# A filler tile in SBUF grows from 192 to 224 bytes per partition, in an fp32r two-layer encoder trunk on one core

## The chip, the cores and the metric

The kernel runs on one core of a Trainium2 chip. The metric is the device time of one execution in microseconds; lower is better. Three runs of the kernel before took 2316.77, 2317.53 and 2318.99 us; their median is 2317.53 us.

## The reference

Two layers of a hybrid block work on 512 frames of width 1024, and a final RMSNorm follows. Each layer normalizes the frames and multiplies them by one wide input matrix. Its columns go to an mLSTM branch (4 heads), a retention branch (4 heads) and two branch gates. The branches are merged and projected; then come a feed-forward part with a squared relu and a gated embedding:

```python
for i in range(DEPTH):
    h = rmsnorm(x, norm1_g[i])
    z = h @ w_in[i] + b_in[i]
    ...                                   # conv, mLSTM and retention, each with its output gate
    merged = jax.nn.sigmoid(gm) * (y_m @ w_bm[i]) + jax.nn.sigmoid(gr) * (y_r @ w_br[i])
    x = x + merged @ w_out[i]
    h2 = rmsnorm(x, norm2_g[i])
    x = x + jnp.square(jax.nn.relu(h2 @ w_ff1[i] + b_ff1[i])) @ w_ff2[i] + b_ff2[i]
    h3 = rmsnorm(x, norm3_g[i])
    x = x + jax.nn.sigmoid(h3 @ w_pe_gate[i]) * (p[i] @ w_pe[i])
return rmsnorm(x, final_g)
```

All of it is float32. The change leaves the computation alone.

## The kernel before

Activations lie with their 1024 features on partitions, in eight tiles of 128 x 512 frames. Every operand of a large product is split into a high part that fp32r holds exactly and a low part (`split`, lines 302 to 304: ScalarE writes the high part, VectorE subtracts it for the low part). Each product is then three matmuls: high by high, high by low, low by high (`mm3`, lines 479 to 482).

The weights arrive as raw pieces `wr` of 128 x 1024 float32 (four buffers), and are split into `wh` and `wl` (six buffers, and two for half-size pieces `wh_D` and `wl_D`). There are four ways in which they are used:

- `t8` (lines 480 to 482): a piece holds eight 128 x 128 blocks. Each block is loaded as TensorE's weights, and a 128 x 512 activation tile is the moving operand. So a matmul has 512 columns.
- `values` (lines 799 to 801): the activations are loaded and 512 columns of the weight piece move.
- `run_pair` (lines 531 to 533): a scheme with seven products in place of eight, on halves of 256 frames. The weights are loaded, 256 columns of activations move. The moving operand is either an activation tile itself or one of the sums that the scheme needs.
- `run_wide` (lines 575 to 577): the same scheme with the operands' roles exchanged. The activations or their sums are loaded, 512 columns of a weight piece move.

A `LDWEIGHTS` on TensorE loads the 128 x 128 operand of the next matmul while a matmul runs; the profile calls it PEld. Most sums of weight pieces are formed in DRAM by transfers that accumulate, issued on GpSimd's queue at a pace tied to the matmuls. Loads of weight pieces go through SP's queue in the order of use.

SBUF is allocated from two ends. The pools of the whole kernel are opened first, on the left (low addresses), in this order:

```python
cpool = pool("const", 1)
cols = pool("cols", 2)
padp = pool("pad", 1)
padp.tile([P, PAD], F32, name="pad")
wpool = pool("w", PIECES)
bpool = pool("big", 1)
opool = pool("one", 1)
```

`pad` is a tile that no instruction touches. The constants and columns end at byte 5,408 of each partition. With `PAD` = 48 floats, 192 bytes, the weight pool begins at 5,600, which is 224 bytes past a multiple of 256. All raw and split pieces are 4,096 or 2,048 bytes long, so each begins 224 bytes past a multiple of 256. So do the tiles of `big` and `one` behind them.

Above them lie the pools of the phases, on the left or on the right (line 976): in layer 0 the activations of a phase (`n1`, `xs`, `n2`, `ns`, `n3`) are on the right, and the working pools (queries and keys, values, `ym`, `yr`, `mh`, the hidden tiles) on the left; in layer 1 it is the other way round. `x`, the high part of the normalized activations `xnh`, and in layer 1 `nsh` lie in `big`, on the left; the low part `xnl` lies in the working pool. The right end of SBUF's allocation is byte 229,344, also 224 past a multiple of 256, and nearly all tiles are multiples of 256 bytes long. So almost every tile on either side begins at 224.

The exception is made by `shift` (lines 275 to 278): it puts a filler of 64 bytes below the sums `xs` and below the feed-forward pool where these are on the left, and one of 192 bytes into the pool where they are on the right. By it the sums `xs` (the moving operand of `l0r`, `l0bgm`, `l0gr` and their like in layer 1, and the loaded operand in the wide units), the hidden tiles `hh` and `hl` (moving in `l0o` and `l1o`) and the embedding's `pth` and `ptl` (moving in `l0pe`) begin 32 bytes past a multiple of 256.

Names in the profile: `l0f` is layer 0's first feed-forward product as whole tiles, `l0f13a` and its like the same product by pairs, `l0o` the second feed-forward product, `l0bm`, `l0br` and `l0wo` the merge and its projection, `l0pg` the gate of the embedding, `l0m` and `l0r` the mLSTM and the retention, `l0g` the retention's output gates.

Of the kernel before, what the change touches and what calls it, by code (L numbers as in the profile page):

```python
# [56 lines left out]
NTMP = 6  # L57
RAWS = 4
PIECES = 3
PAD = 48  # L60
LAST = 4
SIGN = (1.0, -1.0)

# [189 lines left out]
def build(ctx, tc, ins, out):  # L253
# [5 lines left out]
    def pool(name, bufs, **kw):  # L259
        return ctx.enter_context(tc.tile_pool(name=name, bufs=bufs, **kw))  # L260
# [6 lines left out]
# [3 lines that stand above are left out]
# [1531 lines left out]
```

## Time and profile before

| | |
|---|---|
| runs, us | 2316.77, 2317.53, 2318.99; median 2317.53 |
| profiled execution: span, first to last instruction, us | 2313.4 |
| profiled execution: time outside the span | the page gives none |
| instructions | 36,468 |
| TensorE matmul (PE) | 2299.1 us, 99%, 13,532 matmuls |
| TensorE weight load (PEld) | 2035.4 us, 88%, 13,532 loads |
| VectorE (DVE) | 1766.8 us, 76% |
| ScalarE (ACT) | 1269.6 us, 55% |
| GpSimd (POOL) | 624.1 us, 27% |
| granted TensorE clock, mean | 0.998 |
| transfers | 499.36 MB, 187,603 packets, 216 GB/s |

The profile was taken on one execution. Matmuls overlap: one is listed as lasting from its first row to its modelled end, some 390 ns with 512 columns, while the next begins 227 ns after it. So what a matmul costs is read from start to start, and not from its listed duration. Weight loads are listed as PEld. A row of waits names the waiting engine and tile, what it waited for, the total in us, the number of waits and the longest one.

### The profile page before, as it was taken

Reading aid. Unit: us, or ns where it says so; the run is one execution under the profiler, and the core shown is the slowest. Engines: PE = TensorE matmul, PEld = TensorE weight load, DVE = VectorE, ACT = ScalarE, POOL = GpSimd, SP = SyncE. Lnnn points to the kernel's source line nnn. Section 1 sums busy time; section 2 is a strip of 40 time slices with the busy share of each in tenths; the row PEclk is TensorE's granted clock in tenths of the full one; section 3 lists DMA queues with packets and bytes.
Section 4 is the critical chain, followed back from the end, with each engine's and each line's share of the span. In section 5 each row is a group of like instructions: output and inputs, shape, how many; then the busy total and the mean of one; then the engine's idle time right before and its main releaser. Section 6 shows DMA issues by size and latency. Waiting matters only on the chain.

```text
span 2313.4 us, 36468 instructions
## 1 busy us (share of the span) xinstructions
PE 2299.1 (99%) x13532; PEld 2035.4 (88%) x13532; DVE 1766.8 (76%) x2690; ACT 1269.6 (55%) x1837; POOL 624.1 (27%) x984
## 2 busy tenths in 40 slices
PE   9999999999999999999999999999999999999998
PEld 8888899888898899999888888988888888999997
DVE  7878767886676878788778777778867678787785
ACT  6756544644554546556557564445445446566564
POOL 4333222223124322223442332221231242111112
PEclk9999999999999999999999999999999999999999
DMA  7776787777789888888886768877877898878851
GB/s 218 189 191 174 238 228 216 215 227 210 232 230 261 220 228 223 240 239 215 222 224 182 196 174 247 232 216 216 223 221 208 241 266 218 247 232 228 232 160 55
DMA packets 187603, 499.36 MB, mean 216 GB/s; under 512 B 26064, under 2 KB 29520, under 8 KB 187424
## 3 DMA queue, kind: packets, MB, share of 16 engines
q0 software_dynamic: 57520, 188.53, 37.1%
q1 hardware_dynamic: 114496, 281.06, 36.6%
q10 hardware_dynamic: 15408, 27.43, 3.5%
q8 instruction: 106, 1.74, 0.3%
q14 instruction: 73, 0.60, 0.1%
HBM read 478.05 MB, written 194.51 MB: 291 GB/s over the span
## 4 chain that ended last, share of the span: by engine, by line
PE 92%; DVE 5%; ACT 1%; issue 1%; DMA 1%; POOL 0%; SPq 0%; ACTq 0%; DVEq 0%; POOLq 0%
PE l0br L480 1%; PE l1br L480 1%; PE l1br L481 1%; PE l0br L482 1%; PE l1br L482 1%; PE l0br L481 1%; PE l0f L480 1%; PE l0f L481 1%; PE l0f L482 1%; PE l1f L480 1%; PE l1f L481 1%; PE l1f L482 1%; PE l0pg L480 1%; PE l1bm L480 1%; PE l0pg L482 1%
## 5 line engine op out<-in xcount | busy, mean ns | idle before, releaser
L303 ACT ACTIVATE wh<-wr 128x1024 fp32r<-128x1024 f32 (+1 forms) x193 | 199.7, 1041 | 140.5 <-issue 17.1
L304 DVE TENSOR_TENSOR wl<-wr,wh 128x1024 fp32r<-128x1024 f32 (+1 forms) x191 | 234.6, 1230 | 37.5 <-ACT wh L303 36.9
L303 ACT ACTIVATE wh_B<-wr 128x1024 fp32r<-128x1024 f32 x123 | 130.3, 1059 | 184.5 <-PE l0br L481 15.7
L304 DVE TENSOR_TENSOR wl_B<-wr,wh_B 128x1024 fp32r<-128x1024 f32 x123 | 150.3, 1222 | 55.1 <-ACT wh_B L303 50.6
L303 ACT ACTIVATE wh_C<-wr 128x1024 fp32r<-128x1024 f32 x75 | 79.2, 1056 | 69.5 <-PE l0br L481 8.3
L304 DVE TENSOR_TENSOR wl_C<-wr,wh_C 128x1024 fp32r<-128x1024 f32 x75 | 91.7, 1223 | 21.3 <-ACT wh_C L303 17.1
L303 ACT ACTIVATE wh_A<-wr 128x1024 fp32r<-128x1024 f32 x75 | 78.9, 1052 | 44.3 <-DMA wr<-wpairs 5.2
L304 DVE TENSOR_TENSOR wl_A<-wr,wh_A 128x1024 fp32r<-128x1024 f32 x75 | 91.6, 1221 | 12.6 <-ACT wh_A L303 9.4
L303 ACT ACTIVATE wh_D<-wr 128x512 fp32r<-128x512 f32 x75 | 47.2, 630 | 96.5 <-DVE wr L462 27.3
L303 ACT ACTIVATE wh_t<-wr 128x1024 fp32r<-128x1024 f32 x56 | 59.4, 1061 | 69.0 <-PE l0g2va L576 6.0
L304 DVE TENSOR_TENSOR wl_t<-wr,wh_t 128x1024 fp32r<-128x1024 f32 x56 | 68.2, 1221 | 26.1 <-ACT wh_t L303 25.5
L304 DVE TENSOR_TENSOR wl_D<-wr,wh_D 128x512 fp32r<-128x512 f32 x75 | 51.8, 690 | 30.2 <-ACT wh_D L303 28.7
L480 PE MATMUL l0f<-l0n2h,wh 128*128 128x512 f32 x176 | 68.7, 390 | 0.0
L481 PE MATMUL l0f<-l0n2l,wh 128*128 128x512 f32 x176 | 68.6, 390 | 0.0
L482 PE MATMUL l0f<-l0n2h,wl 128*128 128x512 f32 x176 | 68.5, 389 | 0.0
L361 POOL DMA_DIRECT2D s30t<-wpairs x24 | 16.8, 699 | 92.4 <-PE l1o11a L533 9.4
L482 PEld LDWEIGHTS l0f<-l0n2h,wl 128*128 128x128 f32 x176 | 33.0, 188 | 7.0
L480 PEld LDWEIGHTS l0f<-l0n2h,wh 128*128 128x128 f32 x176 | 33.1, 188 | 6.6
L481 PEld LDWEIGHTS l0f<-l0n2l,wh 128*128 128x128 f32 x176 | 33.1, 188 | 6.5
L480 PE MATMUL l1f<-l1n2h,wh 128*128 128x512 f32 x96 | 37.6, 391 | 0.0
L481 PE MATMUL l1f<-l1n2l,wh 128*128 128x512 f32 x96 | 37.5, 390 | 0.0
L482 PE MATMUL l1f<-l1n2h,wl 128*128 128x512 f32 x96 | 37.4, 389 | 0.0
(5797 smaller groups left out, 9132.4 us busy)
## 6 DMA issues: line engine op xcount, KB each, us to landing
wr<-wstream SPq DMA_DIRECT2D x189, 512.0 KB, 4.8
wr<-wpairs SPq DMA_DIRECT2D x225, 256.0 KB, 4.1
wr<-wwide SPq DMA_DIRECT2D x48, 512.0 KB, 4.7
s3t<-wwide POOLq DMA_DIRECT2D x24, 256.0 KB, 5.0
s6t<-wwide POOLq DMA_DIRECT2D x24, 256.0 KB, 5.0
s18t<-wwide POOLq DMA_DIRECT2D x24, 256.0 KB, 4.7
s21t<-wwide POOLq DMA_DIRECT2D x24, 256.0 KB, 5.3
s24t<-wpairs POOLq DMA_DIRECT2D x24, 256.0 KB, 5.7
```

Source lines behind the costliest of these rows:

```text
L303: a = ac.activation(hi_ap, src, AF.Copy)
L304: return a, ve.tensor_sub(lo_ap, src, hi_ap.bitcast(F32))
L361: dma = gp.dma_start(piece(g, x, p, q), piece(g, MADE[x][a], p, q), max_dma_last_dim=4096, **kw)
L480: te.matmul(o, sh, mh, start=first, stop=False)
L481: te.matmul(o, sh, ml, start=False, stop=False)
L482: cur["mm"] = te.matmul(o, sl, mh, start=False, stop=last)
```

## The change

One constant is changed:

```diff
-PAD = 48
+PAD = 56
```

The filler `pad` becomes 224 bytes long. The weight pool begins at byte 5,632, a multiple of 256, and with it all weight pieces, the tiles of `big` and `one`, and all phase pools on the left move up by 32 bytes: what began at 224 past a multiple of 256 begins at 0, and what `shift` had brought to 32 begins at 64. The pools on the right are allocated from the other end and stay at 224 and 32. Constants and columns, below the filler, stay too. Instructions, their order, their waits and their queues are the same.

## The prediction

> **What bounds the kernel now.** I read the busy shares of the page first, then the waits of TensorE's weight loads, then stretches of TensorE work in which nothing waits.
>
> ```profile
> span 2313.4 us, 36468 instructions
> PE 2299.1 (99%) x13532; PEld 2035.4 (88%) x13532; DVE 1766.8 (76%) x2690; ACT 1269.6 (55%) x1837; POOL 624.1 (27%) x984
> PE 92%; DVE 5%; ACT 1%; issue 1%; DMA 1%; POOL 0%; SPq 0%; ACTq 0%; DVEq 0%; POOLq 0%
> ```
>
> TensorE is busy for 2299.1 of 2313.4 us, and the chain that ended last is 92% TensorE. So the time is 13,532 matmuls times the distance between their starts, plus a few waits. The waits of the weight loads, longest first in total:
>
> ```profile
> PEld l1n41ss L718 <- POOL l1n41sum L695: 1.4, 1, 1.4
> PEld l1n41rp L730 <- DVE l1n41d L728: 1.1, 1, 1.1
> PEld warm L961 <- POOL ones_r L292: 1.0, 1, 1.0
> PEld l0gr0a L531 <- DVE l0gr0y L612: 0.8, 1, 0.8
> PEld l1gr0a L531 <- DVE l1gr0y L612: 0.8, 1, 0.8
> ```
>
> The longest are the end of the kernel and its start, and all but those three are under 1 us. A transfer is not among them. What a transfer or a split of a weight piece gains or loses is therefore hidden as long as TensorE finds its piece there.
>
> So I looked at how far apart matmul starts are where TensorE waits for nothing. The next view cuts six such stretches, each from the start of a matmul to the start of another. Its columns are the length, then the busy time of the weight loads with their number, the granted clock, and the transfers' share. A weight load belongs to each matmul and runs beside the matmul before it.
>
> ```profile
> core 0: us, PEld busy (x), PEclk, DMA share, GB/s
> 780.28:823.83 43.55, 36.04 (x192) 1.00 0.81 206
> 267.88:278.61 10.73, 8.60 (x46) 1.00 0.97 309
> 1059.21:1064.72 5.51, 4.51 (x24) 1.00 0.76 256
> 2029.63:2048.34 18.71, 18.70 (x156) 1.00 0.86 235
> 833.35:862.44 29.09, 29.09 (x248) 1.00 0.87 253
> 995.19:1025.90 30.71, 30.71 (x272) 1.00 0.92 254
> ```
>
> In the last two rows one weight load at the edge is counted too; 247 and 271 matmuls begin there. Dividing gives the step from start to start:
> - 780 us, `l0f` (512 columns; moving rows start 224 bytes past a multiple of 256, weights too): 43.55 / 192 = 226.8 ns
> - 267 us, `l0r0v` (512 columns; moving 224, the operand that is loaded as weights 32): 10.73 / 46 = 233.3 ns
> - 1059 us, `l0pe` (512 columns; moving 32, weights 224): 5.51 / 24 = 229.6 ns
> - 2029 us, `l1f13` and `l1f20` (256 columns; 224 and 224): 18.71 / 156 = 119.9 ns
> - 833 us, `l0o` (256 columns; moving 32, weights 224): 29.09 / 247 = 117.8 ns
> - 995 us, `l0o` again, the same addresses: 30.71 / 271 = 113.3 ns
>
> The clock is 1.00 in all of them. Same instruction, same type, same engine: what differs is where the operands start. I call **distance** the start of the moving rows less the start of the weights loaded beside them, modulo 256. 512 columns: 226.8 ns at distance 0, 229.6 at +64, 233.3 at -64. 256 columns: 119.9 at 0, and 117.8 or 113.3 at +64. The two `l0o` rows have equal addresses, so +64 has two steady rhythms, and a stretch can fall into either. Which weight piece or which 512-byte slice it is makes no difference that I find. Distances of +32 or -32 do not occur in this kernel with 256 or 512 columns.
>
> **The change part by part.** No instruction is added or removed; no wait, queue or order is touched. What moves is addresses: everything allocated on the left from the weight pieces on starts 32 bytes higher, everything on the right stays. No tile on the left that ends at the start of one on the right is used in a neighbouring phase, so no new dependency arises from memory that is shared in turn.
>
> *Both operands on the left, or both on the right.* Distance as before. Costed at nothing, except under the second rival.
>
> *One left, one right.* Counted from the program's addresses, the matmuls whose distance changes are:
> - 512 columns, 0 to -32: 1,936. They are the `l0f` and `l0pg` tiles, `l1bm`, `l1br` and `l1wo`, and most of the first `l0m` projections, where the activations lie on the right. Three groups of each carry them:
>
> ```profile
> L480 PE MATMUL l0f<-l0n2h,wh 128*128 128x512 f32 x176 | 68.7, 390 | 0.0
> L481 PE MATMUL l0f<-l0n2l,wh 128*128 128x512 f32 x176 | 68.6, 390 | 0.0
> L482 PE MATMUL l0f<-l0n2h,wl 128*128 128x512 f32 x176 | 68.5, 389 | 0.0
> ```
>
> - 256 columns, +64 to +32: 2,016 (`l1o`, which is 1,344 of them, and the sevenfold sums of layer 0 in `l0r`, `l0bgm`, `l0gr`).
> - 256 columns, 0 to -32: 596 (`l0f` pairs and the low parts of `l1r`, `l1gr`).
> - 512 columns, -64 to -32: 381 (`l0r` and `l0g` wide units, whose sums are the loaded operand).
> - Small: 239 with 512 columns and 194 with 256 columns from 0 to +32, 49 with 512 from +64 to +32.
>
> The price of +-32 has no row. Bounds from the nearest rows, between 0 and 64 on the same side:
> - 512 columns at -32: between 226.8 (distance 0) and 233.3 (-64). It is as near to the one as to the other, so I take the middle, 230.0, +3.2 ns: 1,936 x 3.2 = +6.2 us (ends 0 and +12.6).
> - 256 columns at +32: between 117.8 and 119.9; middle 118.9, +1.1 ns: 2,016 x 1.1 = +2.2 us. The lower end goes below nothing, because the rhythm of 113.3 exists: 2,016 x -4.5 = -9.1 us; the upper end is +2.1 ns, +4.2 us.
> - 256 columns at -32: no row on this side. I take the +3.2 of the 512 columns, 596 x 3.2 = +1.9 us (ends -1.3, if it is like the other side's +64, and +3.9).
> - The wide units go halfway back: 381 x -3.2 = -1.2 us (ends -2.5 and 0).
> - The small groups: 239 x 1.4 - 194 x 1.1 - 49 x 1.4 = +0.1 us.
>
> Sum: 6.2 + 2.2 + 1.9 - 1.2 + 0.1 = **+9.2 us**. All upper ends together give some +21 us, all lower ends some -13 us.
>
> *Transfers into the weight pieces and the splits on ScalarE and VectorE.* The splits read and write tiles that all move by the same 32 bytes:
>
> ```profile
> L303 ACT ACTIVATE wh<-wr 128x1024 fp32r<-128x1024 f32 (+1 forms) x193 | 199.7, 1041 | 140.5 <-issue 17.1
> L304 DVE TENSOR_TENSOR wl<-wr,wh 128x1024 fp32r<-128x1024 f32 (+1 forms) x191 | 234.6, 1230 | 37.5 <-ACT wh L303 36.9
> wr<-wstream SPq DMA_DIRECT2D x189, 512.0 KB, 4.8
> ```
>
> VectorE waits mostly for ScalarE there, and a piece is loaded four buffers ahead. A gain or loss of some per cent of 4.8 us is covered by the wait that the raw piece has for its turn anyway. Costed at nothing. If that cover went, the next to be late would be the split, and it would show as a weight load waiting for `wl`.
>
> The sum is made against the profiled execution: span 2313.4 us, no row gives what lies around it. The median of the runs is 2317.53 us, 4.1 us longer, and nothing in the change touches those 4.1 us. So 2317.5 + 9.2 = 2326.7 us.
>
> **The rivals.**
>
> *Nothing happens (2317.5 us).* The distance would have to be without weight, and the differences above would come from something else that goes with the tile, such as which products follow each other. For it: at +64 one and the same address pair gave 117.8 and 113.3 ns, so the address is not all. Against it: 156 and 247 steps of the same shape differ by 2.1 ns, and the only change between the two stretches is the moving start. The Trainium skill (TensorE: Matmul & The Clock Gate, Part 2, step 1 of the step-by-step) says the same as this rival: TensorE has two independent read ports to SBUF, and loading the next weights takes no read bandwidth from the running matmul. By that rule the sum would be 0; the trace does not agree, 226.8 against 233.3 ns in the first two rows.
>
> *The start itself counts, not the distance: faster (some 2273 us).* Now every operand starts 32 bytes past a multiple of 64 (224 and 32 both do). The steady steps lie in a ladder: 113.3, 119.9, 226.8 and 233.3 are 17, 18, 34 and 35 times 6.67 ns, and 6.67 ns is the time of 64 bytes of moving row: (226.8 - 119.9) / 16 = 6.68, where 16 is the number of 64-byte pieces in 256 columns. A 1,024-byte row that starts in the middle of such a piece touches 17 of them, one that starts on a boundary 16. After the change 4,028 matmuls of 512 columns and 3,980 of 256 columns have a moving row on a 64-byte boundary. If each saves one rung: 8,008 x 6.67 = 53.4 us, so 2326.7 - 53.4 = 2273. For it: the ladder. Against it: no stretch shows a moving row that starts on a boundary, and a fixed gap of one rung between any two matmuls would make the same ladder. It decides wherever both operands lie on the left, as in `l0br` and `l0o`: from about 1.4 ns saved on each of these 8,008 it outweighs the +9.2, and the kernel is faster from 1.8 ns on.
>
> *The right-hand pairs fall into the fast rhythm: faster (some 2306 us).* If +32 gives 113.3 ns, and -32 costs nothing with 512 columns: 2317.5 - 9.1 - 2.5 = 2305.9. For it: the row at 995 us. Against it: the stretch at 833 us has the same addresses and 117.8.
>
> **How the numbers follow.** A step to halfway between measured distances, slower: 0.50, of which 0.05 falls within 0.2% of the time before. Nothing: 0.17. The start itself: 0.18. The fast rhythm: 0.15. 0.2%, 4.6 us, is about what a measurement of this kernel can tell from no change. So faster 0.33, same 0.22, slower 0.45. The time is that of the first case, 2326.7. Its own range, from its bounds without the fast rhythm, is 2318 to 2339. The range for 8 in 10 takes in the fast rhythm and the milder half-way of the second rival: 2298 to 2339; what it leaves out is the full ladder and a +-32 that is worse than both neighbours.
>
> **What would show it.** Cut the same stretches in the profile of the changed kernel. `l0f` (right-hand activations) should step at about 230 ns in place of 226.8, `l1o` at about 119 in place of 117.8, and the wide `l0r0v` at about 230 in place of 233.3. `l0o`, `l0br` and `l1f13`, with both operands on the left, should stand where they are, 117.8, 226.8 and 119.9. If these three fall by up to 6.7 ns, the start itself counts and the second rival is right. If `l1o` steps at 113.3, the third is. Equal steps everywhere are the first. The waits of the weight loads should stay as they are; a new wait for a raw piece or a split would mean that the cover I gave the transfers is gone. The prediction is wrong in sign if -32 is no worse than 0 with 512 columns, since that term is two thirds of the sum.

## The result, and the profile after

The changed kernel takes 2329.81 us (median of 4 runs, 2328.06 to 2330.53). The kernel before took 2317.66 us in the same comparison (4 runs, 2316.77 to 2318.99). The ratio is 1.0053, 95% interval 1.0039 to 1.0067: 12.2 us slower. The forecast was 2326.7.

Span and busy time of the profile after:

```profile
span 2328.8 us, 36468 instructions
PE 2313.8 (99%) x13532; PEld 2036.2 (87%) x13532; DVE 1767.3 (76%) x2690; ACT 1270.6 (55%) x1837; POOL 625.5 (27%) x984
```

PE is busy 14.7 us longer (2299.1 before) and the span is 15.4 us longer; all other engines stand within 1.4 us of where they were. So most of the time is in the matmuls themselves. The longest waits of the weight loads are the same three as before, each within 0.1 us; below are the longest, one that grew by 0.4 us, and the longest one for a split:

```profile
PEld l1n41ss L718 <- POOL l1n41sum L695: 1.5, 1, 1.5
PEld l0r0brqa L531 <- DVE l0r0brqy L612: 1.0, 1, 1.0
PEld l0r2va L576 <- DVE wl_t L304: 0.6, 1, 0.6
```

The last two were 0.6 and 0.3 us before. All waits for splits together, in rows of this kind, went from 1.6 to 3.7 us; a wait for a raw piece is not among them.

The three groups that the prediction showed for `l0f`, 389 or 390 ns each before, now last 395 or 396. The first of them (behind the count: busy time, then the mean ns of one):

```profile
L480 PE MATMUL l0f<-l0n2h,wh 128*128 128x512 f32 x176 | 69.7, 396 | 0.0
```

Stretches without a wait, cut from matmul start to matmul start as before (length, busy time and number of the weight loads, granted clock, the transfers' share). Distance is again the start of the moving rows less the start of the weights loaded beside them, modulo 256:

```profile
core 0: us, PEld busy (x), PEclk, DMA share, GB/s
783.61:828.42 44.81, 36.07 (x192) 1.00 0.79 204
719.34:771.06 51.72, 42.81 (x229) 1.00 0.87 244
270.00:280.72 10.72, 8.64 (x46) 1.00 0.95 294
2045.75:2064.46 18.71, 18.71 (x156) 1.00 0.87 239
889.58:898.09 8.51, 8.50 (x72) 1.00 0.61 157
837.94:867.03 29.09, 29.09 (x249) 1.00 0.89 252
999.91:1031.83 31.92, 31.92 (x272) 1.00 0.89 247
2083.65:2104.50 20.85, 20.85 (x178) 1.00 0.84 248
1877.40:1930.59 53.19, 42.83 (x229) 1.00 0.88 255
```

Where a load at an edge is counted too, the number of matmuls that begin there is 228 (second and last row), 247, 271 and 177. In order of the rows:

- `l0f`, 512 columns, 0 to -32: 44.81 / 192 = 233.4 ns, 226.8 before
- `l0br` and `l0wo`, both operands on the left, distance still 0: 51.72 / 228 = 226.8
- wide `l0r0v`, -64 to -32: 10.72 / 46 = 233.0, 233.3 before
- `l1f13` and `l1f20`, 256 columns, distance still 0: 18.71 / 156 = 119.9, as before
- `l0f13`, 256 columns, 0 to -32: 8.51 / 72 = 118.2
- `l0o`, distance still +64: 29.09 / 247 = 117.8, as before; and 31.92 / 271 = 117.8 in the stretch that ran at 113.3 before
- `l1o`, +64 to +32: 20.85 / 177 = 117.8
- `l1br` and `l1wo`, 512 columns, 0 to -32: 53.19 / 228 = 233.3

To see the whole, I joined every matmul of the two traces with its operands' addresses and summed the steps from start to start by kind. From the first start to the last, the total went from 2304.9 to 2320.8 us, +15.8:

| columns, distance | matmuls | mean step before, after, ns | change, us | forecast, us |
|---|---|---|---|---|
| 512, 0 to -32 | 1,936 | 227.9, 233.6 | +11.0 | +6.2 |
| 256, +64 to +32 | 2,016 | 118.8, 119.4 | +1.2 | +2.2 |
| 256, 0 to -32 | 596 | 119.7, 118.3 | -0.8 | +1.9 |
| 512, -64 to -32 | 381 | 234.1, 235.3 | +0.5 | -1.2 |
| 512, 0 to +32 | 239 | 230.1, 236.0 | +1.4 | +0.3 |
| 256, 0 to +32 | 193 | 128.1, 125.9 | -0.4 | -0.2 |
| 512, still 0 (left) | 2,978 | 228.5, 229.0 | +1.5 | 0 |
| 256, still +64 (left) | 2,013 | 118.7, 119.1 | +0.8 | 0 |

The rows make +15.2; the rest is spread over the other matmuls. Waits are a small part: the 37 steps that changed by more than 30 ns add +1.6 us of the +15.8.

The two profiled executions lie 15.4 us apart, the medians 12.2. The run profiled after took 2330.53 us, 1.7 more than its span. With the same 1.7 the run profiled before took about 2315.1, 2.5 under its median, and the one after was 0.7 over its own. Those 3.2 us lie within the spread between runs of one kernel.

### The profile page after: what moved, and what is told of

Its sections match the earlier page's. It is cut to its first block, busy times and chain, and to the rows that moved or that the text cites. A ratio compares the mean times of both kernels' runs of the same rounds, so it can differ in the third digit from the quotient of the medians.

```text
span 2328.8 us, 36468 instructions
## 1 busy us (share of the span) xinstructions
PE 2313.8 (99%) x13532; PEld 2036.2 (87%) x13532; DVE 1767.3 (76%) x2690; ACT 1270.6 (55%) x1837; POOL 625.5 (27%) x984
## 4 chain that ended last, share of the span: by engine, by line
PE 91%; DVE 5%; ACT 2%; issue 1%; DMA 1%; POOL 1%; DVEq 0%; ACTq 0%; POOLq 0%
PE l0f L480 2%; PE l0f L481 2%; PE l0f L482 2%; PE l1br L481 1%; PE l1br L482 1%; PE l1br L480 1%; PE l0br L480 1%; PE l0br L481 1%; PE l0br L482 1%; PE l1f L480 1%; PE l1f L481 1%; PE l1f L482 1%; DMA wr<-wpairs 1%; PE l0pg L480 1%; PE l0pg L482 1%
```

## The experiments

My theory: the distance alone sets the step, from one matmul's start to the next. The rivals: the place of the operands themselves, the pairs with 256 columns as the cause, and, later, what runs beside TensorE. The first five kernels change allocations alone and run the instructions of the kernel before. In the last two TensorE runs alone with a map of distances.

**Both sides moved.** The 32 bytes are added on the right as well, so that all distances are those of the kernel before and all starts those of the change:

```diff
-PAD = 48
+PAD = 56
+    pool("padr", 1, side="right").tile([P, 56], F32, name="padr")
     wpool = pool("w", PIECES)
```

> The longer filler of the change, and a second filler of 224 bytes at the right end of SBUF, so that right-hand pools also begin at multiples of 256. Every start is 32 bytes further round than in the kernel before, every distance between moving and loaded operand is as before. Theory (the distance counts): back to the time before, 2317.7 us, with l0f at 226.8 ns a step. Rival (the start itself counts: a weight load or an activation that begins at a multiple of 256 is slower): it stays at 2329.8 us or gets worse, since the right-hand operands now begin there too, and l0f stays at 233 ns.

2317.04 us (11 runs) against 2318.81 before (15 runs), ratio 0.9992, 0.9983 to 1.0001. `l0f`, wide `l0r0v`, and `l0o` twice:

```profile
781.20:824.76 43.56, 36.04 (x192) 1.00 0.83 207
268.56:279.30 10.74, 8.65 (x47) 1.00 0.96 304
834.28:863.37 29.09, 29.09 (x248) 1.00 0.89 252
994.92:1025.63 30.71, 30.71 (x272) 1.00 0.90 251
```

43.56 / 192 = 226.9, 10.74 / 46 = 233.5, 29.09 / 247 = 117.8, 30.71 / 271 = 113.3: the steps of before, with every start elsewhere. So with every start 32 bytes further on no cost shows; the loss is in how the operands stand to each other.

**The right side alone moved, the other way.** `PAD` stays at 48, and 32 bytes on the right bring the distances of the change:

```diff
+    pool("padr", 1, side="right").tile([P, 8], F32, name="padr")
     wpool = pool("w", PIECES)
```

> The kernel before with its own filler, and a filler of 32 bytes at the right end, so that the right-hand pools come down by 32 bytes and the weights stay where they were. The distances are those of the changed kernel (-32 for right-hand activations, +32 for right-hand sums and hidden tiles), the weights' starts those of the kernel before. Theory (the distance counts): as slow as the changed kernel, 2329.8 us, with l0f at 233 ns and l0o and l0br unchanged at 117.8 and 226.8. Rival (the weight pieces' start at a multiple of 256 costs the time): 2317.7 us.

2328.37 us (5 runs), ratio 1.0042, 1.0029 to 1.0056. `l0f` and `l0f13`:

```profile
783.59:828.40 44.81, 36.07 (x193) 1.00 0.80 203
888.43:896.96 8.53, 8.52 (x72) 1.00 0.67 201
```

44.81 / 192 = 233.4 and 8.53 / 72 = 118.5. The weight pieces have not moved at all, and the loss is there. So no part of it shows that would need the transfers into them, their splits or the multiples of 256: the ratio is that of the change (1.0053) within the intervals.

**The sums put back.** The change, with the filler of `shift` on the right 32 bytes shorter, so that the sums, the hidden tiles and the embedding's operand are again at +64, and the wide units at -64:

```diff
-PAD = 48
+PAD = 56
-            pl.tile([P, 16 if start else 48], F32, name="shift", tag="shift")
+            pl.tile([P, 16 if start else 40], F32, name="shift", tag="shift")
```

> The changed kernel, with the filler in the right-hand shifted pools 160 bytes long in place of 192, so that right-hand sums and hidden tiles get back their distance of +64 to the weights; right-hand activations stay at -32. Theory (the 512-column steps at -32 are the loss): it stays near the changed kernel; the 2,016 right-hand pair steps were 0.6 ns longer, 1.2 us together, so some 2328 us. Rival (the pairs at +32 carry the loss): back to about 2318 us.

2330.81 us (5 runs), ratio 1.0049, 1.0037 to 1.0062: nothing comes back. The 1,936 steps of 512 columns at -32 make +12.0 us in this run, and 4,029 pairs at +64 step at 119.3 on the mean, no better than the mix of +32 and +64 in the change. The loss is in the 512 columns.

**A map.** `PAD` as before, and the fillers of `shift` so long that the right-hand and left-hand sums and hidden tiles lie at distances that the kernel didn't have:

```diff
-    def shift(pl, side, start):
+    def shift(pl, side, start, to):
         if (side == "left") == start:
-            pl.tile([P, 16 if start else 48], F32, ...)
+            to and pl.tile([P, to if start else 64 - to], F32, ...)
```

The diff is shortened (`...`): the four places that use `shift` give `to` in floats, 48 for the sums of layer 0 and 40 for those of layer 1, 32 for the hidden tiles of layer 0 and 24 for those of layer 1.

> The kernel before, with four other distances in the four shifted groups: l0o at +128, l1o at +96, the sums of layer 1 at +160, those of layer 0 at +192 bytes (wide units: -160 and -192 with 512 columns). It measures the steps at distances that neither kernel has. Theory (any distance but 0 costs 512 columns some 6 ns, and 256 columns gain some 2 ns at any distance but 0): l0o and l1o at 117 to 119 ns, wide units at 230 to 236. Rival (steps grow steadily with the distance up to 128): 256 columns below 115 ns at +96 and +128, wide units above 236 at -160.

2316.94 us in one run, beside the 2318.81 of before; one run settles nothing on the time. Wide `l0r0v` at +64, wide `l1r0v` at +96, `l0o` at +128, `l1o` at +96, and 24 steps of a sum in `l0r1` at -64:

```profile
267.32:277.86 10.54, 8.64 (x46) 1.00 0.93 274
1413.79:1424.53 10.74, 8.64 (x46) 1.00 0.83 210
991.01:1023.16 32.15, 32.15 (x272) 1.00 0.87 241
2149.31:2170.54 21.23, 21.23 (x178) 1.00 0.82 254
372.92:375.66 2.74, 2.74 (x25) 1.00 0.77 205
```

10.54 / 46 = 229.1, 10.74 / 46 = 233.5, 32.15 / 271 = 118.6, 21.23 / 177 = 119.9. With 512 columns there is no slope between near and far: 0 is good, +64 loses 2 ns, and the rest of those measured so far (+96, -32, -64) stands at 233 or more. With 256 columns +96 gains nothing on distance 0 (119.9), where 117 to 119 was expected. The sums of layer 0, now at -64, ran at 2.74 / 24 = 114.2 ns, which I had not expected, and their wide units, now at +64, 4 ns faster than at -64. That asked for the next kernel.

**The fillers of `shift` exchanged.**

```diff
-            pl.tile([P, 16 if start else 48], F32, name="shift", tag="shift")
+            pl.tile([P, 48 if start else 16], F32, name="shift", tag="shift")
```

> The kernel before with the two fillers of shift exchanged (192 bytes on the left, 64 on the right): the sums, the hidden tiles and the embedding's operand lie 64 bytes below the other operands and no longer 64 above. Pair steps with 256 columns go from +64 to -64 (4,032), wide units with 512 from -64 to +64 (764), the embedding with 512 from +64 to -64 (98). Theory A, the distance alone sets the step: the 114.1 ns that the sums of layer 0 showed at -64 hold for all 4,032, 3.6 to 3.7 ns less than the steady 117.8, -14.7 us; the wide units step at 229 for 233.3, -3.3 us; the embedding +0.4 us. Sum -17.6, 2301 us for 2318.8, ratio 0.9924. Rival B, the 114.1 belongs to the sums of layer 0 and to what runs beside them, not to the distance: the hidden products l0o and l1o (2,688 steps) stay at 117.8, the sums alone gain 1,344 x 3.7 = 5.0 us, the wide units 3.3: about 2311 us. Rival C, the rhythm is a matter of chance in each stretch: no steady 114.1 in l1o, a time within 5 us of 2318.8.

2305.35 us (5 runs) against 2318.78 (9 runs), ratio 0.9947, 0.9933 to 0.9960: 13.4 us faster than the kernel before, and faster than both kernels of the comparison. The time lies between theory A and rival B. Wide `l0r2v` at +64; 24 steps of a sum in `l0r1`; `l0o` twice and `l1o` twice, all at -64:

```profile
476.14:486.45 10.31, 8.45 (x45) 1.00 0.68 169
374.98:377.72 2.74, 2.74 (x25) 1.00 0.78 185
831.16:860.25 29.09, 29.09 (x248) 1.00 0.88 249
991.68:1022.41 30.73, 30.73 (x272) 1.00 0.89 253
2059.11:2079.95 20.84, 20.84 (x178) 1.00 0.81 245
2201.71:2228.36 26.65, 26.65 (x236) 1.00 0.59 188
```

10.31 / 45 = 229.1 and 2.74 / 24 = 114.2, as A had it. But the hidden products have both rhythms: 29.09 / 247 = 117.8, 30.73 / 271 = 113.4, 20.84 / 177 = 117.7, 26.65 / 235 = 113.4. So -64 is no fast distance as such. It has the same two rhythms as +64, and more of the stretches fell into the fast one: of the 3,095 places where 12 pair steps at this distance follow each other, 2,090 have a mean step below 115.6 ns, against 493 at +64 in the profile before. With both sides moved, and so with the distances of before, it was 852; so the share is not set by the distance alone. In the profiled run the 4,032 pairs gain 7.4 us and the wide units 2.9. Its span is 9.8 us shorter than that of the profile before, whose run, at about 2315.1, lies some 3.6 us below the median here. The two together make the 13.4.

**TensorE alone.** Two operands of the loaded kind and two moving ones, the moving slice begun d bytes later; 48 matmuls for each d (the loop below twice), and a split running beside the third series:

```python
for j in range(8):
    w = slice(j * P, (j + 1) * P)
    matmul(o, wt[0][:, w], mv[0][:, d // 4:d // 4 + n], ...)   # high by high
    matmul(o, wt[0][:, w], mv[1][:, d // 4:d // 4 + n], ...)   # high by low
    matmul(o, wt[1][:, w], mv[0][:, d // 4:d // 4 + n], ...)   # low by high
```

> No part of the reference is computed: TensorE alone runs 48 matmuls for each distance 0, 32, ... 224 of the moving rows from the loaded operand, with 512 and with 256 columns, in the same pattern of three products; once with rising distances (a), once with falling ones (b), both with no other engine at work and no transfers, and once with rising distances beside a running split on ScalarE and VectorE (c). Theory A, the distance alone sets the step: a, b and c agree and show the map of the large kernel: 512 columns 227 at 0, 229 at 64, 233 to 234 at 32, 96, 128, 192 and 224; 256 columns 120 at 0 and 96, 119 at 32, 118 or 113 at 64, 119 at 128, 118 at 160 and 224, 114 at 192. Rival B, the distance matters only because other engines or transfers use SBUF beside it: a and b step alike at all distances, at the lowest 227 and 113 to 114, and only c differs.

512 columns at 32, 64, 96, 128, 160, 192 and 224 (series a), at 0 (b); then 256 columns at 0, 32, 64, 192, 224 (a), 64, 192 and 32 again (b). 192 is -64 and 224 is -32:

```profile
27.08:38.29 11.21, 9.00 (x49) 1.00 0.00 0
38.29:49.28 10.99, 9.01 (x48) 1.00 0.00 0
49.28:60.50 11.22, 9.02 (x49) 1.00 0.01 1
60.50:71.69 11.19, 9.01 (x48) 1.00 0.00 0
71.69:82.94 11.25, 9.04 (x49) 1.00 0.00 1
82.94:94.13 11.19, 9.02 (x48) 1.00 0.00 0
94.13:105.32 11.19, 9.02 (x48) 1.00 0.00 0
229.04:239.95 10.91, 9.01 (x48) 1.00 0.00 0
105.32:111.06 5.74, 5.74 (x48) 1.00 0.01 3
111.06:116.72 5.66, 5.66 (x49) 1.00 0.00 0
116.72:122.38 5.66, 5.66 (x49) 1.00 0.00 0
139.52:145.17 5.65, 5.65 (x49) 1.00 0.00 0
145.17:150.85 5.68, 5.68 (x49) 1.00 0.00 0
268.17:273.61 5.44, 5.44 (x49) 1.00 0.01 3
245.63:251.10 5.47, 5.47 (x49) 1.00 0.00 0
273.61:279.22 5.61, 5.61 (x49) 1.00 0.00 0
```

Divided by 48. 512 columns: 227.3 at 0, 229.0 at 64, 233.1 to 234.4 at all others. 256 columns: 119.6 at 0, 118.3 at 224; at 64 117.9 and then 113.3; at 192 117.7 and then 114.0; at 32 117.9 and then 116.9. So +64 and -64 are not the only distances with more than one steady step. Transfers stand at 0.00 to 0.01 and no other engine works. Beside the running split, 512 columns at 32 and 224 and 256 at 192 again:

```profile
295.88:307.09 11.21, 9.00 (x49) 1.00 0.00 0
362.93:374.12 11.19, 9.01 (x48) 1.00 0.00 0
408.32:413.97 5.65, 5.65 (x49) 1.00 0.00 0
```

The same to the hundredth of a us as in series a. Rival B falls: the price is there with TensorE alone, and a running split adds nothing to it. That splits on ScalarE and VectorE don't slow TensorE is also what the Trainium skill says (SBUF — State Buffer, "Who interferes with whom").

**What picks the rhythm.** The same loop with 24 matmuls of another kind ahead of each 48 at distance 64 or 192, in short:

```python
for d in (64, 192):
    for n, e in ((256, 0), (256, 32), (256, 96), (256, 128), (256, 160), (256, 224), (512, 0), (512, 32)):
        cell(n, e, 24)      # the entry: n columns at distance e
        cell(256, d, 48)
```

> No part of the reference is computed: TensorE alone runs 48 matmuls of 256 columns at distance 64 (then 192) after 24 matmuls of another kind: 256 columns at distance 0, 32, 96, 128, 160 or 224, 512 columns at 0 or 32, and once after a wait for VectorE; all twice (a, b); then 288 in a row at 64 and at 192 after 512 columns at 0. Theory A, at these two distances there are two steady rhythms, 117.7 and 113.4 to 114.1 ns, and how the stretch is entered picks one: the same entry gives the same rhythm in a and b, 117.7 after 32 and 160 as in the run before, 113.4 or 114.0 after 96 and 224, and the long stretches keep the rhythm that they begin with to their end. Rival B, the rhythm drifts by chance: a and b differ for the same entry, and the long stretches change rhythm on the way.

256 columns at 192 after 224, and after 160; at 64 after 512 columns at 32, and at 0; and 264 of the long stretch at 192:

```profile
140.61:146.08 5.47, 5.47 (x49) 1.00 0.02 3
132.12:137.77 5.65, 5.65 (x49) 1.00 0.00 0
84.63:90.07 5.44, 5.43 (x48) 1.00 0.01 3
73.39:79.05 5.66, 5.66 (x48) 1.00 0.00 0
375.40:406.49 31.09, 31.09 (x264) 1.00 0.00 1
```

114.0, 117.7, 113.3, 117.9, and 31.09 / 264 = 117.8. The entry decides, and the long stretches kept their rhythm throughout. The second round repeated the first for all entries but one, 256 columns at 32 ahead of 64 (117.8, then 113.8); there some matmuls of the following cells had been ordered ahead of a wait, so that the entry was not quite the same. That this is why is not shown. My list of which entry gives which rhythm was wrong in three of eight: at 64, 96 and 224 gave 117.8 and not 113.4, and at 192, 32 gave the fast rhythm and not 117.7. 512 columns at 32, for which I had no guess, gave the fast one at both distances. A rule for it I don't have.

## Why the prediction was right, and where it was off

*The mechanism* held in the main. Little moved in waits, transfers or splits: the waits for splits grew by 2.1 us in all, none is longer than 0.6, and the cover that the prediction gave the transfers was not used up. Raw pieces land 4.7 us after their issue (4.8 before), now that they start on multiples of 256:

```profile
wr<-wstream SPq DMA_DIRECT2D x189, 512.0 KB, 4.7
```

The stretches in which no distance changed stayed (226.8, 119.9, 117.8), but for rhythm; those of `l0f`, `l1br` and `l0f13` moved with theirs. Slower was the forecast's likeliest case. That its +9.2 comes near the 12.2 is in part luck: the largest term was 4.8 us too small, two terms had the wrong sign, and a term put at nothing made +2.3 in the profiled runs.

*512 columns, 0 to -32*: mis-sized, +6.2 for +11.0. The step that failed is "as near to the one as to the other, so I take the middle". It took the step to rise evenly with the distance; the lone matmuls show that it doesn't: 227.3 at 0, and at 32 from it, on either side, 233.1 to 233.5, like the 233.1 at -64. The upper end of the range (+12.6) was the answer. The same error made 239 steps at +32 +1.4 us instead of +0.3.

*Wide units, -64 to -32*: wrong in sign, +0.5 for -1.2, and for the same reason: "halfway back" was nowhere, 233.0 against 233.3 in the stretch.

*256 columns, 0 to -32*: wrong in sign, -0.8 for +1.9. I had carried the price of 512 columns over. With 256 columns distance 0 is one of the dearest, 119.6 against 118.3 at -32, as the row at +64 on the other side hinted (its end, -1.3, stood in the range).

*256 columns, +64 to +32*: near in size, +1.2 for +2.2, but not for the reason given. In the profile after, `l1o` steps at 117.8, not at the 118.9 that I interpolated; that is the slow rhythm of +64. Before, of 1,223 places in `l1o` where 12 such steps follow each other, 197 were in the fast rhythm (mean below 115.6 ns), and none is after the change; `l1o` makes +0.5 of the +1.2. Another 0.7 are two single steps, in `l0r0brk` and `l0gr`, that waited longer.

*Left with left*: put at nothing, and the profiled runs show +1.5 and +0.8. The +1.5 is an effect of neighbours, which the prediction did not have. Of the 2,978 steps with 512 columns, 548 stand next to a step whose distance changed; they went from 231.8 to 235.1 ns, +1.8 us. The other 2,430 went from 227.8 to 227.6, -0.3 us. In the 548 the kernel that moved the right side alone shows +1.9 us and the one with the sums put back +2.0; the one that moved both sides shows -0.2. The loss is in layer 1, where the high part `l1xnh` lies on the left and the low part `l1xnl` on the right, so that one matmul in three changes its distance. `l1m2o`, 48 steps, in the profile before and in the one after:

```profile
1356.89:1367.79 10.90, 9.01 (x49) 1.00 0.44 124
1365.70:1376.89 11.19, 9.01 (x50) 1.00 0.46 131
```

That is 227.1 and 233.1 ns. The 16 steps of the low part, now at -32, went from 227.8 to 233.9, but the 32 of the high part, still at 0, went from 226.9 to 232.7 too. So the distance of a step alone does not set its length, as my theory had it; that of the steps beside it counts as well.

For the pairs it is the rhythm: the 271 steps of `l0o` that went from 113.3 to 117.8 make 271 x 4.5 = 1.2 us with unchanged distances, more than the whole +0.8.

*The rivals.* "Nothing happens" falls with the kernel that moved the right side alone. With it falls, for this pair of operands, the rule of the Trainium skill that it leaned on (TensorE: Matmul & The Clock Gate, "Step-by-step: what each phase is for"): two independent read ports for weights and moving rows. 227.3 against 233.1 ns with TensorE alone says that how the two starts stand to each other costs time; where the two reads meet, no run here shows. "The start itself counts" falls with the kernel that moved both sides: 2317.04 us. "The fast rhythm" needed two things. A free -32 with 512 columns is not so; 113 ns at +32 with 256 was not seen as a steady step (117.8 in the kernel; 117.9 and 116.9 with TensorE alone).

*The time around the span.* I put 4.1 us of the median down to what lies around the span. In the profile after it is 1.7; the rest was a run below its median. That changed nothing in the sum.

*Two slips in the working.* 9.2 us over 8,008 matmuls is 1.15 ns each, where the second rival has 1.4. And the bounds without the fast rhythm end at 2317.5 - 1.3 - 2.5 = 2313.7 us, where the prediction has 2318. Neither bears on the forecast.

## What to carry to other kernels

Where a kernel is bound by the steps between matmuls, the start of the moving tile against the start of the weights loaded beside it, modulo 256, is worth choosing: with fp32r operands here, equal for 512 columns, 64 apart in either direction for 256, and with 512 columns the same for all matmuls that follow each other. Before interpolating between two measured addresses, measure the one in question: a loop of 48 matmuls on TensorE alone gave the whole map in one run, and the big kernel followed it in the stretches where all steps have one distance. A steady step that differs between stretches with equal addresses is a state that the entry picked, not a property of the address.

## What the runs showed of the hardware

- The distance has no slope with 512 columns: 227.3 ns at 0, 229.0 at +64, 233.1 to 234.4 at the six other multiples of 32.
- A step at distance 0 loses time beside steps at another distance: in `l1m2o`, where one of three went to -32, the other two went from 226.9 to 232.7 ns.
- 256 columns at +64 and at -64 have two steady rhythms each, 117.9 and 113.3, 117.7 and 114.0. What ran ahead picks one (15 of 16 entries gave the same one twice), and it lasted for 264 steps without a change.
- The price of a distance needs no other engine and no transfer: beside a running split the lone matmuls stepped the same to 0.01 us in 48.
- Exchanging two fillers, 192 and 64 bytes, made the kernel 13.4 us faster; the 32 bytes of this change made it 12.2 us slower.
